# A hybrid encoder layer: first loads in smaller pieces, shorter routing, and eleven lower weight parts on GpSimd

## Chip, cores and metric

The kernel runs on one core of one Trainium2 chip. The metric is the device time of one execution in microseconds (us). Engines are named TensorE (PE; PEld is its weight load), VectorE (DVE), ScalarE (ACT), GpSimd (POOL) and SyncE (SP), which issues nearly all the DMA transfers here.

## The reference, cut to what matters

One layer over 256 tokens of 2048 float32 values. A projection of the normed input feeds a gated causal convolution (31 taps, 1024 channels) and a differential attention (8 heads); both go through an output projection and are added to the input. Then each token is routed to one of 4 groups and there to 2 of 8 experts.

```python
u = rms_norm(h, norm1_g) @ w_in                     # 2048 x 5120
y_conv = conformer_conv(u[..., :2048], ...)         # a * sigmoid(b), 31 taps, layer norm, silu
y_attn = diff_attention(u[..., 2048:], ...)         # chunk mask, softmax(0) - lam * softmax(1)
h = h + concat([y_conv, y_attn]) @ w_out            # 2048 x 2048
t = rms_norm(h, norm2_g)
g_idx = argmax(t @ w_group + b_group)
top_v, top_i = top_k((t @ w_router + b_router)[g_idx], 2)
for e in range(32):
    out += combine[:, e:e + 1] * ((silu(t @ w_gate[e]) * (t @ w_up[e])) @ w_down[e])
return h + out
```

## The kernel before

**Front part.** The input projection has 80 steps and the output projection 32, numbered 0 to 111. A step has 256 rows of the contraction and 512 output columns for both token tiles (128 tokens each). Both operands are split into an upper part, rounded to fp32r, and a lower part, the rest; a step is twelve products of 128x512, three for each block of 128 rows and each token tile: upper by upper (L721), upper by lower weight (L722), lower by upper weight (L723). `split` makes a step's weight parts: ScalarE copies the upper part (L672), VectorE subtracts for the lower (L673). There are three buffers for them (`SP`, pairs 18 to 20), and `split` runs two steps ahead of the products. For the first eight steps it also splits two blocks of x (`split_x`, L263).

The work that depends on a finished projection stands in small generators ("units": gated products and conv taps, keys, queries, values, attention, its norm, conv norm and output). The program's order on TensorE, ScalarE, VectorE and GpSimd is the order in which the code is written: ahead of each step `vector_phase` lets units run on ScalarE and VectorE, as far as a room in microseconds for each engine lasts (`PACE_A`, `PACE_V`), and fills VectorE's room with conv taps, `TAP` = 0.40 each; behind each step `tensor_phase` lets units put products on TensorE. Where a step needs a unit that is not done, `idle_until` (L248) runs phases with room `IDLE` and two filler products each. Two such places matter: step 88, the second half of attention in the output projection, and step 96, where the conv output enters it.

```python
room["D"] = min(room["D"], SAVE) + d + room["P"]
fill(room["D"] - sum(u["n"][1] for u in units if may(u, "D")))
```

**Routing.** `finish` adds the last output parts, transposes the result and multiplies it by the router. Then VectorE picks group and experts (L764 to L789), TensorE counts positions, and `dispatch` (L847) builds one-hot matrices that gather tokens into 64 slots an expert.

**Expert stage.** 16 pairs of experts; each pair's gate, up and down weights come in 12 transfers of 2 MB through a ring of nine buffers (`E_RING`), which are those of the front part, and a transfer is issued when its buffer has been read.

Of the kernel before, what the change touches and what calls it, by code (L numbers as in the profile page):

```python
# [9 lines left out]
F32 = mybir.dt.float32  # L10
# [3 lines left out]
U32 = mybir.dt.uint32  # L14
# [22 lines left out]
IDLE = 2.5  # L37
# [5 lines left out]
WARM, WARM2 = 12, 3  # L43
SAVE, NTMP, NORM1_AT = 0.0, 6, 5
# [13 lines left out]
def block_kernel(ctx, tc, x, xT, par, w_in, w_out, w_gu, w_dn, out):  # L58
# [22 lines left out]
    nc.scalar.dma_start(pr[:, p1:], par[:, p1:])  # L81
# [22 lines left out]
    xs = cst.tile([128, NT, D], F32, name="xs")  # L104
    for t in range(NT):
        nc.sync.dma_start(xs[:, t], x[t * 128:(t + 1) * 128])
    win += [stream(IN_PAIRS[2], w_in[2])]
# [18 lines left out]
    place = cst.tile([128, NT, EPG], U32, name="place")  # L126
    nc.gpsimd.iota(place, pattern=[[0, NT], [1, EPG]], base=0, channel_multiplier=0)
# [3 lines left out]
    nc.vector.memset(eps_c, EPS)  # L131

# [107 lines left out]
    def keep_warm(n):  # L240

        if n and free_banks:
            i, ps = bank()
            for _ in range(n):
                nc.tensor.matmul(ps[:, :128], ident, ident, start=True, stop=True)
            free_banks.append(i)

    def idle_until(done):  # L248
# [3 lines left out]
        while not done():  # L252
            vector_phase(IDLE, IDLE)
            keep_warm(IDLE_MM)
# [178 lines left out]
    def queries(half, ps):  # L433
# [4 lines left out]
        for t in range(NT):  # L438
            yield "A", 1.3, 2
# [53 lines left out]
    def attend(t, g, s, st):  # L493
# [15 lines left out]
        for r in range(2):  # L509
            yield "D", 1.0, 0  # L510
            b0, v = pv[r]
            nc.vector.memset(v[0:64, :, K - 64:K], NEG)
# [706 lines left out]
```

## Time and profile before

| what | value |
|---|---|
| time, median of 3 runs (lowest to highest) | 1305.32 us (1304.71 to 1306.32) |
| the profiled execution's own time | 1305.24 us |
| its span | 1303.3 us |
| TensorE busy | 1231.6 us, 94% |
| VectorE, ScalarE, GpSimd busy | 515.6, 291.7, 46.8 us |
| first expert product | 385.59 us |
| DMA rate, mean over the span | 360 GB/s |

Times inside the profile count from the span's start. A busy time is the union of an engine's instructions; products overlap in the pipeline, so TensorE's pace is read from the distance of their starts. Lines (L672) are those of the kernel before; the changed kernel's numbers differ.

### The profile page before, as it was taken

To read this page: it belongs to the slowest core of one execution; us is meant where nothing else is said; L and a number is where in the kernel's file an instruction comes from. 1 tells how busy PE (TensorE), PEld (TensorE's weight loads), DVE (VectorE), ACT (ScalarE), POOL (GpSimd) and SP (SyncE) were. 2 spreads that over 40 slices of the span, in tenths; PEclk is the share of its full clock that TensorE was granted. 3 is DMA by queue.
4 is the path that set the end of the run, shared out by engine and by line. 5 is a ranking of instruction groups with operands and counts; after the bars stand their busy time and mean duration, and the time that the engine had idled before them with its cause. 6 is when DMAs were issued, how large, how long until landed. Compare 5 with 4: busy or idle time off the path is not lost.

```text
span 1303.3 us, 15071 instructions
## 1 busy us (share of the span) xinstructions
PE 1231.6 (94%) x6291; PEld 700.8 (54%) x6291; DVE 515.6 (40%) x996; ACT 291.7 (22%) x516; POOL 46.8 (4%) x116
## 2 busy tenths in 40 slices
PE   7999999989999999999999898999989898998997
PEld 5888888878884353553535435252525344352533
DVE  6899989897541030330303213030303123030313
ACT  6446565645421010110101101010101001010101
POOL 1001211120000000000000000000000000000000
PEclk9999999989999999999999999999999999999999
DMA  9454534665749999999999999999999999999996
GB/s 385 173 184 180 194 137 187 256 260 212 273 183 420 426 426 429 427 427 426 429 427 428 427 427 428 427 428 427 427 426 430 426 428 425 429 428 427 427 426 246
DMA packets 37032, 469.29 MB, mean 360 GB/s; under 512 B 4192, under 2 KB 4960, under 8 KB 8160
## 3 DMA queue, kind: packets, MB, share of 16 engines
q1 hardware_dynamic: 35808, 466.63, 86.1%
q10 hardware_dynamic: 1152, 1.65, 0.4%
q8 instruction: 51, 0.84, 0.3%
q14 instruction: 21, 0.17, 0.0%
HBM read 466.17 MB, written 2.10 MB: 359 GB/s over the span
## 4 chain that ended last, share of the span: by engine, by line
PE 65%; DMA 31%; DVE 2%; ACT 1%; POOL 1%; issue 0%; SPq 0%
DMA v<-in_w_gu_dram 28%; PE b L891 13%; PE b L929 13%; PE b L872 8%; PE b L722 7%; PE b L723 7%; PE b L721 7%; PE b L956 4%; DMA v<-in_w_dn_dram 3%; PE b L505 1%; PE b L633 1%; PE b L907 0%; ACT t L430 0%; DMA v<-in_w_in_dram 0%; PE b L561 0%; DVE u L673 0%
## 5 line engine op out<-in xcount | busy, mean ns | idle before, releaser
L891 PE MATMUL b<-v,u 128*64 128x512 f32 x2048 | 452.5, 594 | 45.4 <-DMA v<-in_w_gu_dram 45.3
L891 PEld LDWEIGHTS b<-v,u 128*64 128x64 f32 x2048 | 142.8, 137 | 349.7 <-issue 264.4
L900 DVE TENSOR_TENSOR hid<-sil,b 64x512 f32<-64x512 f32 x32 | 21.9, 685 | 517.5 <-ACT sil L899 517.4
L929 PE MATMUL b<-v,hT 128*64 128x512 f32 x992 | 217.2, 594 | 1.3 <-DMA v<-in_w_dn_dram 0.8
L721 PE MATMUL b<-u,v 128*128 128x512 f32 x448 | 179.0, 400 | 8.4 <-ACT u L672 8.4
L722 PE MATMUL b<-u,v 128*128 128x512 f32 x448 | 175.6, 392 | 1.1 <-DVE u L673 1.1
L723 PE MATMUL b<-u,v 128*128 128x512 f32 x448 | 175.7, 392 | 0.0
L673 DVE TENSOR_TENSOR u<-v,u 128x1024 fp32r<-128x1024 f32 x112 | 137.4, 1228 | 47.1 <-ACT u L672 46.7
L672 ACT ACTIVATE u<-v 128x1024 fp32r<-128x1024 f32 x112 | 119.0, 1063 | 140.3 <-PE b L723 108.9
L929 PEld LDWEIGHTS b<-v,hT 128*64 128x64 f32 x992 | 69.7, 137 | 134.2 <-issue 131.6
L899 ACT ACTIVATE sil<-b,sv 64x512 f32<-64x512 f32 x32 | 21.8, 682 | 527.7 <-PE b L891 503.1
L872 PEld LDWEIGHTS b<-dg,xs 128*128 128x128 f32 x1024 | 121.1, 192 | 14.7 <-issue 11.7
L872 PE MATMUL b<-dg,xs 128*128 128x128 f32 x1024 | 125.5, 276 | 0.5 <-ACT hT L909 0.2
L937 ACT ACTIVATE u<-b,sv 128x512 fp32r<-128x512 f32 (+1 forms) x66 | 44.4, 674 | 244.5 <-PE b L929 193.3
L721 PEld LDWEIGHTS b<-u,v 128*128 128x128 f32 x448 | 84.9, 189 | 25.2 <-ACT u L672 8.4
L325 DVE SCALAR_TENSOR_TENSOR v<-v,pr 128x255 f32<-128x255 f32 (+14 forms) x240 | 97.1, 464 | 0.0
L722 PEld LDWEIGHTS b<-u,v 128*128 128x128 f32 x448 | 84.8, 189 | 18.9 <-DVE u L673 2.2
L723 PEld LDWEIGHTS b<-u,v 128*128 128x128 f32 x448 | 84.6, 189 | 17.9
L938 DVE SCALAR_TENSOR_TENSOR u<-b,sv,u 128x512 fp32r<-128x512 f32 (+1 forms) x66 | 48.2, 732 | 109.4 <-ACT u L937 109.4
L956 PE MATMUL b<-u,dwT 128*128 128x512 f32 (+2 forms) x264 | 76.7, 412 | 0.3 <-DVE u L957 0.3
L874 DVE TENSOR_TENSOR u<-b,g2v 128x512 f32<-128x512 f32 x64 | 44.3, 692 | 29.7 <-PE b L872 29.2
L957 DVE TENSOR_TENSOR u<-u,b 128x512 f32<-128x512 f32 (+2 forms) x62 | 41.2, 664 | 29.6 <-PE b L956 29.6
(202 smaller groups left out, 553.7 us busy)
## 6 DMA issues: line engine op xcount, KB each, us to landing
v<-in_w_gu_dram SPq DMA_DIRECT2D x125, 2048.0 KB, 32.5
v<-in_w_dn_dram SPq DMA_DIRECT2D x60, 2048.0 KB, 34.7
v<-in_w_in_dram SPq DMA_DIRECT2D x18, 2048.0 KB, 8.0
v<-in_w_out_dram SPq DMA_DIRECT2D x8, 2048.0 KB, 8.6
v<-in_w_gu_dram SPq DMA_DIRECT2D x6, 1024.0 KB, 12.3
v<-in_w_dn_dram SPq DMA_DIRECT2D x5, 1024.0 KB, 8.0
v<-in_w_in_dram SPq DMA_DIRECT2D x8, 512.0 KB, 8.9
v<-in_xT_dram SPq DMA_DIRECT2D x4, 512.0 KB, 8.5
```

What stands on the lines that cost most here:

```text
L325: nc.vector.scalar_tensor_tensor(cacc[:, b, d:], hb[:, b, :S - d], ck[:, b, j:j + 1], cacc[:, b, d:], op0=ALU.mult, op1=ALU.add)
L672: nc.scalar.activation(sp[:, 0], w, AF.Copy)
L673: nc.vector.tensor_tensor(sp[:, 1], w, sp[:, 0].bitcast(F32), op=ALU.subtract)
L721: nc.tensor.matmul(o, lh, sp[:, 0, k2], start=first and k2 == 0, stop=False)
L722: nc.tensor.matmul(o, lh, sp[:, 1, k2], start=False, stop=False)
L723: nc.tensor.matmul(o, ll, sp[:, 0, k2], start=False, stop=last and k2 == 1)
L872: nc.tensor.matmul(tv[:, k], xs[:, t, (k0 + k) * 128:(k0 + k + 1) * 128], dg[:, t].rearrange("p i c -> p (i c)"), start=t == 0, stop=t == 1)
L891: nc.tensor.matmul(gu[i][h:h + 64], tT[:, kb, i * C:(i + 1) * C], w[:, k2, g], start=kb == 0, stop=kb == KB - 1, skip_group_check=True)
L929: nc.tensor.matmul(ps[64 * i:64 * i + 64], hT[:, f, i], columns(wd[i], f), start=f == 0, stop=f == 3, skip_group_check=True)
L937: nc.scalar.activation(y[:, 0, a:b], ps[:, :b - a], AF.Copy, scale=sv[:, 0:1])
L938: nc.vector.scalar_tensor_tensor(y[:, 1, a:b], ps[:, :b - a], sv[:, 0:1], y[:, 0, a:b].bitcast(F32), op0=ALU.mult, op1=ALU.subtract)
L956: nc.tensor.matmul(ps[:, :b - a], dwT[:, t], y[:, k, a:b], start=k == 0, stop=k == 1)
```

## The change

1. First loads: x comes in two pieces of 0.26 MB for the first four blocks; the second part of the parameters moves from ScalarE's queue to SyncE's, behind the weights of step 3; the third weight pair comes in halves around x itself. ScalarE's table load is put ahead of the data by a dummy instruction. Eleven filler products stand ahead of the first step. Step 0's weight parts are made in two halves.
2. Eleven lower parts (steps 14, 16, ..., 34) are made by GpSimd. From step 12 to 69 `split` runs three steps ahead, and from step 11 to 73 the buffer of the conv output (`CY`) gives two more buffers for weight parts.
3. The first norm starts at step 9 instead of 5. Idle turns give VectorE 1.3 instead of 2.5. The mask is filled by ScalarE; the squares of the first half of the queries are summed by ScalarE.
4. The last two steps run by token tile, so that tile 0 is transposed earlier.
5. Routing works on all 32 experts' logits with a penalty for the groups not chosen, instead of first picking 8; `dispatch` builds its four one-hot blocks by one instruction.

The core of the diff:

```diff
+WARM0, WARM, WARM2 = 11, 12, 3
+POOL_STEPS, MORE_AT = range(14, 36, 2), 11
+SAVE, NTMP, NORM1_AT = 0.0, 6, 9
...
-    nc.scalar.dma_start(pr[:, p1:], par[:, p1:])
...
     for q in range(4):
-        nc.sync.dma_start(xT_s[:, 4 * q:4 * q + 4], xTv[:, 4 * q:4 * q + 4])
         for p in range(2):
             cs = slice(p * 1024, (p + 1) * 1024)
+            if q == 0:
+                nc.sync.dma_start(xT_s[:, 2 * p:2 * p + 2], xTv[:, 2 * p:2 * p + 2])
+            elif p == 0:
+                nc.sync.dma_start(xT_s[:, 4 * q:4 * q + 4], xTv[:, 4 * q:4 * q + 4])
             nc.sync.dma_start(win[q // 2][:, q % 2, cs], w_in[q // 2][:, q % 2, cs])
+        if q == 1:
+            nc.sync.dma_start(pr[:, p1:], par[:, p1:])
...
+    nc.scalar.activation(dummy, eps_c, AF.Copy)
...
+            vector_phase(IDLE, IDLE_V)
+            keep_warm(warm)
...
-            nc.vector.memset(v[0:64, :, K - 64:K], NEG)
+            nc.scalar.activation(v[0:64, :, K - 64:K], mean_w[0:64, None, :64].to_broadcast([64, nh, 64]), AF.Copy,
+                                 scale=NEG * DC)
...
+        if j == MORE_AT:
+            cs = pair(CY, [128, 2, 2, 2, 512], F32R)
+            for i in range(2):
+                more_sp.append(cs[:, i])
+                last_user["c", i] = -9
+        i = min([i for i in last_user if (i != SP[0] or j < 96) and (i in SP or j < 74)], key=lambda x: last_user[x])
...
+        if j == 0:
+            for k2, kb in enumerate(kx):
+                split_x(kb)
+                nc.scalar.activation(sp[:, 0, k2], w[:, k2], AF.Copy)
+                nc.vector.tensor_tensor(sp[:, 1, k2], w[:, k2], sp[:, 0, k2].bitcast(F32), op=ALU.subtract)
+        else:
+            nc.scalar.activation(sp[:, 0], w, AF.Copy)
+            eng = nc.gpsimd if j in POOL_STEPS else nc.vector
+            if eng is nc.gpsimd:
+                room["D"] += 1.22
+            eng.tensor_tensor(sp[:, 1], w, sp[:, 0].bitcast(F32), op=ALU.subtract)
...
+    keep_warm(WARM0, mean_w)
...
+            if MORE_AT < j < 70:
+                ahead = 3
...
+            if j >= len(steps) - 2:
+                if j == len(steps) - 2:
+                    products(j, [0])
+                    products(j + 1, [0])
...
-    nc.vector.tensor_tensor(pick, lg[:, :, NG:].rearrange("p t (g e) -> p t g e", g=NG), goh4, op=ALU.mult)
-    nc.vector.tensor_reduce(el, pick.rearrange("p t g e -> p t e g"), axis=AX.X, op=ALU.add)
+    nc.vector.tensor_scalar(goh, goh, -1.0, -NEG, op0=ALU.add, op1=ALU.mult)
+    nc.vector.tensor_tensor(el.rearrange("p t (g e) -> p t g e", g=NG), lg[:, :, NG:].rearrange("p t (g e) -> p t g e", g=NG),
+                            goh[:, :, :, None].to_broadcast([128, NT, NG, EPG]), op=ALU.add)
...
-        for t in range(NT):
-            for i in range(2):
-                nc.vector.tensor_scalar(dg[:, t, i], slots, pc(t, i), None, op0=ALU.is_equal)
+        nc.vector.tensor_tensor(dg, slots[:, None, None, :].to_broadcast([128, NT, 2, C]),
+                                pc[:, :, :, None].to_broadcast([128, NT, 2, C]), op=ALU.is_equal)
```

How it moves instructions, at three places. On VectorE, around the gated products of the third half of the gate (steps 24 to 26). Before: L673 is a step's lower part, L325 a conv tap, L338 a gated product.

```order
L673 TENSOR_TENSOR u_648<-v_429,u_648 128x1024
L325 SCALAR_TENSOR_TENSOR v_121<-v_121,pr 128x233 x2
L325 SCALAR_TENSOR_TENSOR v_121<-v_121,pr 128x232 x2
L673 TENSOR_TENSOR u_673<-v_429,u_673 128x1024
L325 SCALAR_TENSOR_TENSOR v_121<-v_121,pr 128x231 x2
L338 SCALAR_TENSOR_TENSOR t_655<-b_494,rstd_118,t_655 128x256
L338 SCALAR_TENSOR_TENSOR t_657<-b_495,rstd_118,t_657 128x256
L673 TENSOR_TENSOR u_694<-v_511,u_694 128x1024
```

And now, where these are L706, L334 and L347, up to the lower part of step 29:

```order
L706 TENSOR_TENSOR v_341<-v_416,v_341 128x1024
L334 SCALAR_TENSOR_TENSOR v_124<-v_124,pr 128x238
L334 SCALAR_TENSOR_TENSOR v_124<-v_124,pr 128x237 x2
L334 SCALAR_TENSOR_TENSOR v_124<-v_124,pr 128x236 x2
L334 SCALAR_TENSOR_TENSOR v_124<-v_124,pr 128x235
L347 SCALAR_TENSOR_TENSOR t_660<-b_502,rstd_121,t_660 128x256
L347 SCALAR_TENSOR_TENSOR t_662<-b_503,rstd_121,t_662 128x256
L706 TENSOR_TENSOR u_698<-v_493,u_698 128x1024
```

Every second lower part is gone from VectorE, and six to eight taps stand between two of those that are left.

On VectorE, in the wait ahead of step 88, behind the rsqrt of the last attention norm; L591 and L593 scale the attention output (L577 and L579 before), L602 makes its lower part (L588), L615 adds an output part (L601), L379 subtracts the conv mean (L370). Now:

```order
L615 TENSOR_TENSOR xs<-xs,b_2395 128x512
L591 TENSOR_TENSOR oy<-oy,rs_2254 128x4
L593 TENSOR_TENSOR t_2460<-b_2270,oy 128x512
L591 TENSOR_TENSOR oy<-oy,rs_2286 128x4
L593 TENSOR_TENSOR t_2466<-b_2408,oy 128x512
L334 SCALAR_TENSOR_TENSOR v_124<-v_124,pr 128x230
L334 SCALAR_TENSOR_TENSOR v_124<-v_124,pr 128x229 x2
L334 SCALAR_TENSOR_TENSOR v_124<-v_124,pr 128x228 x2
L334 SCALAR_TENSOR_TENSOR v_124<-v_124,pr 128x227 x2
L602 SCALAR_TENSOR_TENSOR v_1663<-b_2471,qg,v_1663 128x4x128
L334 SCALAR_TENSOR_TENSOR v_124<-v_124,pr 128x226
L602 SCALAR_TENSOR_TENSOR v_1663<-b_2484,qg,v_1663 128x4x128
```

Before, all taps stood ahead of the second tile's scaling, and the conv mean was subtracted ahead of its lower part; now the last tap and the subtraction stand behind it.

On ScalarE, the conv output ahead of step 96. Before: L387 loads a table behind the root of the conv variance, L672 is a step's upper part (here of steps 91 to 93), L407 and L408 make the output of the first of four channel groups.

```order
L387 ACT_TABLE_LOAD
L387 ACTIVATE dummy<-eps_c 128x1
L672 ACTIVATE u_2548<-v_2077 128x1024
L672 ACTIVATE u_2571<-v_2201 128x1024
L672 ACTIVATE u_2590<-v_2201 128x1024
L407 ACTIVATE v_121<-v_121,pr 128x256 x2
L408 ACTIVATE v_2558<-v_121 128x512
```

And now (L396, L701, L416, L417; L395 is the root), with the upper parts of steps 95 and 96:

```order
L395 ACTIVATE t_2600<-b_2586,eps_c 128x256
L396 ACT_TABLE_LOAD
L396 ACTIVATE dummy<-eps_c 128x1
L701 ACTIVATE u_2619<-v_2199 128x1024
L701 ACTIVATE u_2658<-v_2337 128x1024
L416 ACTIVATE v_124<-v_124,pr 128x256 x2
L417 ACTIVATE v_2629<-v_124 128x512
```

Before, the other groups followed with the upper parts of steps 94 and 95 between them; now the three others follow at once, and behind them stands the upper part of step 97.

## Rows read from the trace of the kernel before

**Rows 1.** Busy time by stretch: columns PE, PEld, DVE, ACT, POOL, clock, DMA, GB/s

```profile
17.88:279.60 261.72, 261.29 (x1230) 218.07 (x1229) 235.29 (x460) 152.68 (x295) 36.54 (x91) 1.00 0.55 209
281.00:295.68 14.68, 9.18 (x50) 8.23 (x48) 12.15 (x27) 7.15 (x17) 4.62 (x13) 0.77 0.41 150
295.68:370.14 74.46, 74.43 (x365) 62.05 (x364) 44.63 (x57) 36.81 (x50) 0.00 (x0) 1.00 0.61 230
390.00:1280.00 890.00, 841.07 (x4368) 380.40 (x4366) 191.98 (x361) 78.86 (x126) 0.00 (x0) 1.00 1.01 427
```

**Rows 2.** Time line of SyncE's queue, DMA issues (start, us, what)

```profile
370.48 0.43 SPq L991 DMA_DIRECT2D v<-in_w_gu_dram  x1
...
387.59 5.46 SPq L989 DMA_DIRECT2D v<-in_w_dn_dram  x4
```

**Rows 3.** Time line of the start (start, us, engine, line, what, count, idle before)

```profile
4.80 1.28 ACT L265 ACT_TABLE_LOAD   x1 [4.80 <-DMA v<-in_xT_dram]
...
6.10 0.91 ACT L265 ACTIVATE v<-v,pr 128x256 fp32r<-128x256 f32 x2
...
7.29 1.06 ACT L672 ACTIVATE u<-v 128x1024 fp32r<-128x1024 f32 x1 [0.29 <-DMA v<-in_w_in_dram]
...
8.40 0.80 PE L721 MATMUL b<-u,v 128*128 128x512 f32 x1 [8.40 <-ACT u L672]
...
10.28 0.80 PE L722 MATMUL b<-u,v 128*128 128x512 f32 x1 [1.08 <-DVE u L673]
...
15.11 0.39 PE L721 MATMUL b<-u,v 128*128 128x512 f32 x1
...
17.88 0.39 PE L721 MATMUL b<-u,v 128*128 128x512 f32 x1
```

**Rows 4.** Time line, GpSimd and VectorE at once

```profile
7.99 1.15 POOL L301 TENSOR_TENSOR pr<-pr 128x576 f32<-128x576 f32 x1 [2.70 <-DMA pr<-in_par_dram]
...
8.38 1.84 DVE L673 TENSOR_TENSOR u<-v,u 128x1024 fp32r<-128x1024 f32 x1 [0.86 <-ACT u L672]
...
108.79 1.23 DVE L673 TENSOR_TENSOR u<-v,u 128x1024 fp32r<-128x1024 f32 x1 [0.27 <-ACT u L672]
108.90 1.20 POOL L148 TENSOR_TENSOR kh<-kh,kv 128x16 f32<-128x16 f32 x1
...
113.92 0.22 POOL L148 TENSOR_TENSOR kh<-kh,kv 128x16 f32<-128x16 f32 x1
```

**Rows 5.** Time line, VectorE's taps, a gated product and TensorE's transposes

```profile
53.42 1.64 DVE L325 SCALAR_TENSOR_TENSOR v<-v,pr 128x250 f32<-128x250 f32 x4
...
84.55 0.87 DVE L338 SCALAR_TENSOR_TENSOR t<-b,rstd,t 128x256 f32<-128x256 f32 x2
...
86.82 0.60 PE L346 MATMUL b<-ident,t 128*128 128x128 f32 x4
```

**Rows 6.** Time line ahead of step 88 (L721 from 295.68 is its first product)

```profile
279.57 1.05 PE L561 MATMUL b<-v,t 128*128 128x128 f32 x8
...
287.90 2.07 PE L366 MATMUL b<-v,mean_w 128*128 128x256 f32 x4 [5.50 <-DVE v L325]
...
292.41 3.62 PE L381 MATMUL b<-t,mean_w 128*128 128x256 f32 x16
...
293.76 0.75 DVE L588 SCALAR_TENSOR_TENSOR v<-b,qg,v 128x512 fp32r<-128x512 f32 x1 [1.27 <-ACT v L586]
...
295.68 0.58 PE L721 MATMUL b<-u,v 128*128 128x512 f32 x1
```

**Rows 7.** Time line, conv output on VectorE and ScalarE

```profile
301.39 1.74 DVE L390 RECIPROCAL t<-t 128x256 f32<-128x256 f32 x1
...
306.29 1.09 ACT L407 ACTIVATE v<-v,pr 128x256 f32<-128x256 f32 x2 [0.95 <-DVE v L403]
...
307.41 0.63 ACT L408 ACTIVATE v<-v 128x512 fp32r<-128x512 f32 x1
```

**Rows 8.** Time line, one-hot builds ahead of the first gather

```profile
377.60 1.39 DVE L852 TENSOR_SCALAR dg<-slots,pos 128x64 f32<-128x64 f32 x8
```

More of the change, by code (lines that the diff above doesn't have):

```diff
@@ L125, in block_kernel @@
                    allow_small_or_imprecise_dtypes=True)
-    place = cst.tile([128, NT, EPG], U32, name="place")
-    nc.gpsimd.iota(place, pattern=[[0, NT], [1, EPG]], base=0, channel_multiplier=0)
+    place = cst.tile([128, NT, NE], U32, name="place")
+    nc.gpsimd.iota(place, pattern=[[0, NT], [1, NE]], base=0, channel_multiplier=0)
     dummy = cst.tile([128, 1], F32, name="dummy")
@@ L244, in keep_warm, with idle_until @@
             for _ in range(n):
-                nc.tensor.matmul(ps[:, :128], ident, ident, start=True, stop=True)
+                w = ident if w is None else w
+                nc.tensor.matmul(ps[:, :128], w, w, start=True, stop=True)
             free_banks.append(i)
-    def idle_until(done):
+    def idle_until(done, warm=IDLE_MM):
         nonlocal now
@@ L715, in block_kernel, with products @@
                 ps[pk] = [bank() for _ in range(NT)]
-            for k2 in range(2):
-                for t in range(NT):
-                    ts = slice(t * 128, (t + 1) * 128)
-                    o, sp = ps[pk][t][1], halves[j]
-                    lh, ll = lhs[0][:, kb0 + k2, ts], lhs[1][:, kb0 + k2, ts]
-                    nc.tensor.matmul(o, lh, sp[:, 0, k2], start=first and k2 == 0, stop=False)
-                    nc.tensor.matmul(o, lh, sp[:, 1, k2], start=False, stop=False)
-                    nc.tensor.matmul(o, ll, sp[:, 0, k2], start=False, stop=last and k2 == 1)
+            def products(j, tiles):
+                _, _, kb0, _, pk, first, last = steps[j]
+                for k2 in range(2):
+                    for t in tiles:
+                        ts = slice(t * 128, (t + 1) * 128)
+                        o, sp = ps[pk][t][1], halves[j]
+                        lh, ll = lhs[0][:, kb0 + k2, ts], lhs[1][:, kb0 + k2, ts]
+                        nc.tensor.matmul(o, lh, sp[:, 0, k2], start=first and k2 == 0, stop=False)
+                        nc.tensor.matmul(o, lh, sp[:, 1, k2], start=False, stop=False)
+                        nc.tensor.matmul(o, ll, sp[:, 0, k2], start=False, stop=last and k2 == 1)
+            if j >= len(steps) - 2:
+                if j == len(steps) - 2:
+                    products(j, [0])
+                    products(j + 1, [0])
+                    tensor_phase(2)
+                    now += 1
+                    start(finish(pk[2], 0, ps[pk][0]), 1, quick=True)
+                else:
+                    products(j - 1, [1])
+                    tensor_phase(0)
+                    now += 1
+                    vector_phase(PACE_A, PACE_V)
+                    products(j, [1])
+                    tensor_phase(0)
+                    now += 1
+                    start(finish(pk[2], 1, ps[pk][1]), 1, quick=True)
+                continue
+            products(j, range(NT))
             tensor_phase(2)
@@ L747, in block_kernel @@
         nc.scalar.activation(dummy, eps_c, AF.Sqrt)
-        idle_until(lambda: not units)
+        idle_until(lambda: not units, 0)
     keep_warm(WARM)
```

75 lines of the change are left out of this document (33 added, 42 removed).

## The prediction

> **What bounds the kernel now.** I read the busy times by stretch first, then SyncE's queue, then the time line of three places: the start, the wait ahead of the output projection's second part, and the routing. From 390 us to 1280 us the DMA engines are busy all the time (share 1.01, 427 GB/s), and TensorE has pauses (841 of 890 us) [rows 1]. So the expert stage runs at the pace of its weights, whatever an engine does in it. What starts that stream? SyncE issues the last transfer for which there is a free buffer at 370.48, and the next at 387.59 [rows 2], when the first expert products have read their first buffer. From there the stream never stops. So every microsecond by which the front part ends earlier comes off the end, one for one, and nothing in the expert stage itself can add to it.
>
> In the front part TensorE is the bound. From 17.88, where the third step of the input projection (step 2) begins, to 279.6 it is busy 261.29 of 261.72 us, and from 295.68 to 370.14 for 74.43 of 74.46; VectorE has 235.29 us in the first of these stretches [rows 1], which is nearly full, but it is in time. In between lies the one hole: 281.0 to 295.68, where TensorE is busy 9.18 us at a granted clock of 0.77, and much of that is filler. So the change can win time at the start (17.9 us for two steps), in the hole, and in the routing. Between 17.88 and 279.6 it can only lose.
>
> **The start.** Before, ScalarE waits until 4.80 for the first 0.52 MB of x and then loads its table for 1.28; the first weights let it go at 7.29, the first product stands at 8.40, the second waits for VectorE until 10.28, then the products start 0.44 apart (11 intervals to 15.11), and step 2 begins at 17.88, the products now 0.23 apart (12 from 15.11 to 17.88) [rows 3]. [...]
>
> Changed: the table load stands ahead of the data, the second parameter load (0.59 MB) behind the weights of step 3, and x comes in 0.26 MB pieces. Ahead of the first weights' last byte there are now 0.80 MB instead of 1.65; at 427 GB/s [rows 1] this is 2.0 us, so they land at 7.29 - 2.0 = 5.3. The small parameter load on ScalarE's queue is as before, so I leave ScalarE's first product at 4.80. Then: scaling of one x block 0.46 (half of 0.91 [rows 3]), copy of half a weight tile 0.6 (half of 1.06 and a little), the same again, and step 1 with 0.91 + 1.06: its copy ends at 8.9. VectorE's lower part, 1.23 [rows 5], ends at 10.15. There step 1's second product starts, 11 more at 0.23 follow, and step 2 begins at 12.8 instead of 17.88: **-5.1**. This takes TensorE at the high level from step 0 on: eleven filler products run from 1.3 to 6.0 (each is recorded as two of 128 columns, together one of 256, and four of those took 2.07 with the last one's tail at the low level [rows 6], 0.43 each); before, TensorE ran from 10.28 to 15.11 until its level rose. Bounds: -6.0 if the parameters land sooner, -3.5 if the level rises only in step 1 (some 8 products at 0.2 more).
>
> **Eleven lower parts on GpSimd.** TensorE did not wait for lower parts, so nothing is won directly; the question is what GpSimd costs VectorE. No row shows a 1024-wide subtraction on GpSimd. The nearest: 128x576 took 1.15, and a 128x16 one 0.22 [rows 4], so 1.65 ns an element and 1.9 us for 1024. [...]
>
> Next, both engines at once. VectorE's lower part that started at 8.38 while GpSimd's 128x576 ran until 9.14 took 1.84 instead of 1.23; and a GpSimd instruction of 0.22 took 1.20, because VectorE's lower part from 108.79 ended at 110.02 [rows 4]. So one stands still while the other reads two inputs. [...]
>
> With that, the move takes 1.23 off VectorE and puts 1.9 of standing still on it, eleven times in 22 steps. Does TensorE see it? The first place is the transposes of the third gated half ahead of step 27, which need two VectorE results; before, these were ready 1.4 us early (84.55 + 0.87 against 86.82) [rows 5]. By the new order VectorE has, from its first conv tap (behind the transposes ahead of step 14) to there, 43 taps of 0.39, five lower parts of 1.2, four gated products of 0.44 and 6 or 7 stops of 1.9: 16.8 + 6.0 + 1.8 + 12.4 = 37.0. TensorE needs 13 steps of 2.72 and four transposes, 35.8, less 1.7 until the first tap: 34.1. VectorE is 2.9 late; some of the stops fall into its gated products, which read one input from PSUM and need not stop, so I take **+2.0**. Three steps of lead and five buffers keep the products themselves supplied (TensorE is three steps, 8.2 us, behind). Bounds: 0 (no stop) and +6 (2.5 us each, and again at the keys ahead of step 37).
>
> Nor do more taps get done for it: the credit that each moved part gives is cut to zero ahead of the next step's taps, as room is limited to SAVE = 0. By the order 68 taps stand ahead of the lower part of step 36 where 80 stood before, partly as the first norm starts at step 9 instead of 5.
>
> **The hole and the conv output.** Before, the last attention product group starts at 279.57 and step 88 at 295.68. Useful work in the hole: L366 0.9 (2.07 at the low level), L381 3.5, four transposes 0.4 [rows 6], so 14.7 - 4.8 = 9.9 are lost. In the new order the last group stands one step earlier, and VectorE has behind its squares: four taps, two adds, the rsqrt (on GpSimd, 12 instructions of 0.22 [rows 4] and the step to the next, 3.4), two 512-wide products, seven taps, the low part of the first tile, a tap, the low part of the second. With 0.39 a tap and 0.7 for 512 wide [rows 5, 6] the low parts stand 12.9 and 14.1 after the group's start, step 88, whose third and sixth products need them, ends at 15.7, and without waiting it would end at 7.2: 8.5 lost. Now the variance products (L390, L381 before) stand ahead of step 92 and no longer ahead of step 88, so the conv output has four steps (10.9) to step 96 where it had eight. VectorE's reciprocal stands behind the lower part of step 95, whose upper part waits for the buffer of step 92: it starts 5.6 after the variance. Reciprocal and Newton take 3.1, the first scaling 0.65 [rows 7], so ScalarE begins at 9.3; then all four groups, 1.7 each, stand on ScalarE ahead of the upper part of step 97. Low part of group 0: 13.6, step 96 waits 2.4. Upper part of 97: 9.3 + 6.8 + 1.1 = 17.2, lower 18.4, where it was wanted at 16.3: 2.1 more. Sum 8.5 + 4.5 - 9.9 = **+3.1**. Bounds: -4 (the conv output hidden, a shorter rsqrt) and +5.
>
> **End of the front part.** The four one-hot builds ahead of the first gather, half of 1.39 [rows 8], become one of 128x256, 0.44 as the gated product of that size [rows 5]: -0.26. Of the routing two 64-wide instructions of some 0.25 go, one comes, and four read 64 or 32 elements instead of 16 or 8: -0.1. The last two steps by token tile: tile 0 is transposed 0.44 earlier and delays the last product by as much; VectorE's chain behind it is the same: 0. Together **-0.4** (0 to -1).
>
> **At nothing:** the squares of half the queries (1.6 more on ScalarE each, 0.7 less on VectorE) and the mask's fill on ScalarE, which has 153 of 262 us [rows 1]; were ScalarE late, TensorE would wait up to 2 us at step 50. Fewer taps in idle turns is in the walk above. The 15 later one-hot builds lie beside the stream.
>
> **Sum:** -5.1 + 2.0 + 3.1 - 0.4 = -0.4. The profiled execution took 1305.24, the median is 1305.32: forecast **1304.8**, no change that a measurement can tell (0.2% is 2.6 us).
>
> **Rivals.** *GpSimd does not stop VectorE, and the conv output fits (faster).* Its reads fall into VectorE's pauses (10% of that stretch [rows 1]), and the upper part of step 97 finds ScalarE free. Then 2.0 and 4.5 go: 1298.3. For it: GpSimd's short instructions cost VectorE's taps nothing visible. Against it: the 1.84.
>
> *The stop is longer (slower).* Writing fp32r and reading two full inputs, a part takes 3.0 us on GpSimd; VectorE is then 6.5 x 1.1 = 7.2 later at step 27, and TensorE waits there for the gated products: 1312.0. It decides from 2.4 us a part on, where 6.5 x 0.5 = 3.3 more give 1308.1; at 2.6 it is 1309.4. [...]
>
> *The start gives less.* If the level stays low through step 1 and the weights land late, the start brings -2.5: 1307.4, still within 0.2%.
>
> *The change does what it says:* freed time on VectorE closes the conv early and the hole shrinks to the rsqrt, 5 us: 1305.2 - 5.1 + 2.0 - 5 - 0.4 = 1296.7. The order speaks against it: 225 taps stand ahead of the lower part of step 86, 228 before.
>
> **Chances.** Forecast 0.36, faster rival 0.32, slower 0.18, weak start 0.08, early conv 0.06. So faster 0.38, same 0.44, slower 0.18. The range takes in the early conv, and the slower rival to 2.6 us a part: 1296.5 to 1309.5.
>
> **What would show it.** Step 2 beginning at 12 to 14 us; GpSimd's parts near 1.9 us and VectorE's instructions beside them longer by about that; a wait of TensorE ahead of step 27 for a gated product; waits at steps 88, 96 and 97 of 8, 2 and 2 us; the first expert product less than 1 us earlier. It is wrong if the hole is under 5 us, if GpSimd's parts take over 2.6, or if the expert stage's stream is interrupted.

## The result and the profile after

The changed kernel takes **1311.95 us** (median of 4 runs, 1311.29 to 1313.16) against 1305.01 of the kernel before in the same measurement: ratio 1.0054, 95% interval 1.0042 to 1.0067. It is slower by 7 us. The forecast was 1304.8 with a range up to 1309.5, so it was wrong in sign and outside its range. The profiled execution took 1311.9, its span is 1310.1 (1303.3 before).

First the busy times by stretch, for the same four stretches as [rows 1] (step 2 to the hole, the hole, step 88 to the end of the output projection, the expert stage). Columns as there: length, then PE, PEld, DVE, ACT, POOL busy, clock, DMA share, GB/s.

```profile
13.47:283.57 270.10, 265.70 (x1243) 220.38 (x1242) 242.14 (x443) 160.91 (x348) 70.78 (x100) 0.99 0.56 215
283.57:292.18 8.61, 4.83 (x24) 4.35 (x23) 5.82 (x17) 2.00 (x3) 3.36 (x17) 0.69 0.42 170
292.18:374.99 82.81, 78.93 (x374) 65.09 (x374) 49.46 (x64) 38.98 (x55) 0.00 (x0) 0.97 0.53 194
398.00:1290.00 892.00, 842.81 (x4375) 381.29 (x4372) 188.11 (x319) 78.87 (x126) 0.00 (x0) 1.00 1.01 427
```

The last line is as before: the stream of expert weights runs without a break, and what the front part loses is lost at the end. The other three differ. TensorE, which had 0.43 us of idle time in the first stretch before (261.29 of 261.72 busy), now has 4.4 us. VectorE, from which eleven instructions were taken, is busy 242 us instead of 235 (in a stretch 8 us longer). And behind the hole TensorE is idle for 3.9 of 82.8 us, where it was idle for 0.03 of 74.5.

**The start** (time line, rows of ScalarE and TensorE), to be held against [rows 3]:

```profile
1.19 1.28 ACT L139 ACT_TABLE_LOAD   x1 [1.19 <-PEq L1259]
...
5.91 0.63 ACT L698 ACTIVATE u<-v 128x512 fp32r<-128x512 f32 x1 [0.92 <-DMA v<-in_w_in_dram]
...
6.60 0.68 PE L761 MATMUL b<-u,v 128*128 128x512 f32 x1 [0.32 <-ACT u L698]
...
10.80 0.50 PE L762 MATMUL b<-u,v 128*128 128x512 f32 x1 [0.42 <-DVE u L706]
...
13.47 0.39 PE L761 MATMUL b<-u,v 128*128 128x512 f32 x1
```

Step 2 begins at 13.47 instead of 17.88, with products 0.23 apart from step 0 on. That is 4.4 us sooner (forecast 5.1). The weights let ScalarE go at 5.91, where the prediction had 5.3.

**GpSimd's parts** (time line of GpSimd, VectorE and TensorE; L706 is the lower part, L347 the gated product, L334 a tap, L355 the transposes of a gated half):

```profile
43.25 2.42 POOL L706 TENSOR_TENSOR u<-v,u 128x1024 fp32r<-128x1024 f32 x1 [28.19 <-ACT u L701]
45.62 3.36 POOL L706 TENSOR_TENSOR v<-v,v 128x1024 fp32r<-128x1024 f32 x1
...
56.51 2.45 POOL L706 TENSOR_TENSOR u<-v,u 128x1024 fp32r<-128x1024 f32 x1 [4.18 <-ACT u L701]
60.14 2.50 POOL L706 TENSOR_TENSOR v<-v,v 128x1024 fp32r<-128x1024 f32 x1 [1.18 <-ACT v L701]
70.10 4.28 POOL L706 TENSOR_TENSOR u<-v,u 128x1024 fp32r<-128x1024 f32 x1 [7.47 <-ACT u L701]
...
44.15 2.60 DVE L706 TENSOR_TENSOR u<-v,u 128x1024 fp32r<-128x1024 f32 x1 [1.67 <-ACT u L701]
46.67 0.86 DVE L347 SCALAR_TENSOR_TENSOR t<-b,rstd,t 128x256 f32<-128x256 f32 x2
...
56.62 6.68 DVE L334 SCALAR_TENSOR_TENSOR v<-v,pr 128x252 f32<-128x252 f32 x6
63.22 0.86 DVE L347 SCALAR_TENSOR_TENSOR t<-b,rstd,t 128x256 f32<-128x256 f32 x2
...
47.20 0.83 PE L355 MATMUL b<-ident,t 128*128 128x128 f32 x4 [0.93 <-DVE t L347]
...
63.75 0.83 PE L355 MATMUL b<-ident,t 128*128 128x128 f32 x4 [2.07 <-DVE t L347]
...
65.17 0.63 PE L761 MATMUL b<-u,v 128*128 128x512 f32 x1
...
68.53 0.39 PE L763 MATMUL b<-u,v 128*128 128x512 f32 x1
```

Read the sixth row with the first: VectorE's lower part starts at 44.15, while GpSimd's first part runs, and takes 2.60 instead of 1.23 [rows 4]. Behind it on VectorE stand the two gated products, and TensorE waits 0.93 for them ahead of step 14. The six taps from 56.62 take 6.68 instead of some 2.5 (four took 1.64 in [rows 5]), because two parts of GpSimd (56.51 and 60.14) fall into them; the next gated products start at 63.22, and TensorE waits 2.07 ahead of step 19. After that wait its products start 0.43 apart from 65.17 to 68.53 (granted clock 0.64 from 63.7 to 68.5): eight intervals take 3.36 where they take 1.82 at 0.227, another 1.5 us. The part at 70.10 shows the other side: five taps of VectorE run end to end, and GpSimd's part takes 4.28.

Before the change, VectorE's results for the transposes ahead of step 19 were ready at 63.22, 1.4 us before TensorE came to them (L338 is the gated product, L346 the transposes):

```profile
62.35 0.87 DVE L338 SCALAR_TENSOR_TENSOR t<-b,rstd,t 128x256 f32<-128x256 f32 x2
...
64.59 0.60 PE L346 MATMUL b<-ident,t 128*128 128x128 f32 x4
```

**The hole and the conv output** (time line, TensorE and VectorE; L575 the last product group of attention, L429 the transposes of its normalised output, L375 the second part of the conv's mean, L390 its variance, L399 the reciprocal, L419 a low part of the conv's output):

```profile
279.27 1.05 PE L575 MATMUL b<-v,t 128*128 128x128 f32 x8
...
287.34 1.11 PE L429 MATMUL b<-ident,t 128*128 128x128 f32 x4 [3.38 <-DVE t L593]
...
296.38 1.02 PE L375 MATMUL b<-v,mean_w 128*128 128x256 f32 x4
...
305.46 3.62 PE L390 MATMUL b<-t,mean_w 128*128 128x256 f32 x16
...
312.94 1.23 DVE L706 TENSOR_TENSOR u<-v,u 128x1024 fp32r<-128x1024 f32 x1 [3.53 <-ACT u L701]
...
314.42 1.75 DVE L399 RECIPROCAL t<-t 128x256 f32<-128x256 f32 x1
...
322.47 0.50 PE L763 MATMUL b<-u,v 128*128 128x512 f32 x1 [1.58 <-DVE v L419]
...
326.00 0.50 PE L761 MATMUL b<-u,v 128*128 128x512 f32 x1 [0.97 <-ACT u L701]
...
327.26 0.50 PE L762 MATMUL b<-u,v 128*128 128x512 f32 x1 [0.76 <-DVE u L706]
```

In [rows 6] the mean and the variance stood inside the hole. Now the mean stands behind step 88, the variance ahead of step 92, the reciprocal behind VectorE's lower part at 312.94. TensorE waits for the conv's low part in step 96 (1.58) and for both parts of step 97's weights (0.97 and 0.76).

**The tail**: the first gather's two one-hot builds, and the issue that starts the stream.

```profile
385.40 0.76 DVE L902 TENSOR_TENSOR dg<-slots,pos 128x256 f32<-128x256 f32 x2
```

```profile
395.29 3.74 SPq L1040 DMA_DIRECT2D v<-in_w_dn_dram  x3
```

The two builds take 0.76 where eight took 1.39 [rows 8]. The issue that waits for the first expert products starts at 395.29 instead of 387.59 [rows 2]: 7.7 us later, and the stream follows.

### The profile page after: what moved, and what is told of

Its sections match the earlier page's. It is cut to its first block, busy times and chain, and to the rows that moved or that the text cites. A ratio compares the mean times of both kernels' runs of the same rounds, so it can differ in the third digit from the quotient of the medians.

```text
span 1310.1 us, 15097 instructions
## 1 busy us (share of the span) xinstructions
PE 1239.9 (95%) x6305; PEld 705.5 (54%) x6305; DVE 512.5 (39%) x922; ACT 297.5 (23%) x560; POOL 79.0 (6%) x127
## 4 chain that ended last, share of the span: by engine, by line
PE 58%; DMA 32%; DVE 6%; ACT 1%; issue 1%; POOL 1%; SPq 0%; ACTq 0%; DVEq 0%
DMA v<-in_w_gu_dram 28%; PE b L942 13%; PE b L980 13%; PE b L923 8%; PE b L763 5%; PE b L762 5%; PE b L761 5%; PE b L1007 4%; DMA v<-in_w_dn_dram 3%; DVE v L334 2%; DMA v<-in_w_in_dram 2%; DVE u L706 1%; PE b L517 1%; ACT u L701 1%; PE b L958 0%
## 5 line engine op out<-in xcount | busy, mean ns | idle before, releaser
L761 PE MATMUL b<-u,v 128*128 128x512 f32 x344 | 139.5, 406 | 1.3 <-ACT u L701 1.0
L763 PE MATMUL b<-u,v 128*128 128x512 f32 x344 | 135.6, 394 | 2.1 <-DVE v L419 1.6
L762 PE MATMUL b<-u,v 128*128 128x512 f32 x344 | 135.9, 395 | 1.2 <-DVE u L706 1.2
L706 DVE TENSOR_TENSOR u<-v,u 128x1024 fp32r<-128x1024 f32 x78 | 100.9, 1296 | 45.6 <-ACT u L701 45.6
L701 ACT ACTIVATE u<-v 128x1024 fp32r<-128x1024 f32 x85 | 89.8, 1062 | 87.7 <-PE b L763 78.3
L334 DVE SCALAR_TENSOR_TENSOR v<-v,pr 128x255 f32<-128x255 f32 (+14 forms) x240 | 109.3, 515 | 0.0
L763 PEld LDWEIGHTS b<-u,v 128*128 128x128 f32 x344 | 65.4, 190 | 17.3 <-DVE v L419 2.0
L762 PEld LDWEIGHTS b<-u,v 128*128 128x128 f32 x344 | 65.7, 191 | 15.2 <-DVE u L706 1.9
L761 PEld LDWEIGHTS b<-u,v 128*128 128x128 f32 x344 | 65.5, 190 | 14.6 <-ACT u L701 1.4
## 6 DMA issues: line engine op xcount, KB each, us to landing
v<-in_w_in_dram SPq DMA_DIRECT2D x2, 1024.0 KB, 13.6
```

The source lines that it names most:

```text
L334: nc.vector.scalar_tensor_tensor(cacc[:, b, d:], hb[:, b, :S - d], ck[:, b, j:j + 1], cacc[:, b, d:], op0=ALU.mult, op1=ALU.add)
L701: nc.scalar.activation(sp[:, 0], w, AF.Copy)
L706: eng.tensor_tensor(sp[:, 1], w, sp[:, 0].bitcast(F32), op=ALU.subtract)
L761: nc.tensor.matmul(o, lh, sp[:, 0, k2], start=first and k2 == 0, stop=False)
L762: nc.tensor.matmul(o, lh, sp[:, 1, k2], start=False, stop=False)
L763: nc.tensor.matmul(o, ll, sp[:, 0, k2], start=False, stop=last and k2 == 1)
```

## The experiments

Each kernel was run with the kernel before on the same chip. The tables give its median, and by how much the first product of a step of the projections starts later (+) or sooner (-) on TensorE than before the change, one trace against one trace.

| kernel | median us | ratio, 95% | step 12 | 20 | 80 | 88 | 92 | 100 |
|---|---|---|---|---|---|---|---|---|
| the change | 1311.95 | 1.0042 to 1.0067 | -4.88 | +0.99 | +2.38 | -3.49 | +1.94 | +7.86 |
| e1 no part on GpSimd | 1306.49 | 1.0005 to 1.0023 | -5.36 | -4.19 | -4.26 | -8.67 | -5.19 | +2.42 |
| e2 old norm and room | 1315.96 | 1.0070 to 1.0097 | +0.54 | +5.72 | +7.78 | +6.42 | +12.07 | +11.55 |
| e3 start alone | 1305.16 | 0.9993 to 1.0011 | -0.30 | -0.30 | -0.31 | -0.02 | -0.02 | 0.00 |
| e4 GpSimd alone | 1310.50 | 1.0026 to 1.0054 | -0.71 | +4.80 | +6.01 | +4.71 | +4.68 | +4.71 |

Theory A was what the trace of the change suggested: GpSimd's parts cost 6 to 7 us, the rest of the loss is the conv output. Theory B: the parts cost nothing, the later first norm, the shorter idle turns and the squares on ScalarE do.

**e1, the change without parts on GpSimd**

```diff
-POOL_STEPS, MORE_AT = range(14, 36, 2), 11
+POOL_STEPS, MORE_AT = (), 11
```

> The changed kernel with all lower parts on VectorE again; everything else stays, the two extra buffers and the three steps of lead too. Theory A (GpSimd's parts cost some 6 to 7 us: the waits ahead of steps 14 and 19, the low level after them and the keys; the rest of the loss is the conv output): 1305 to 1307 us, step 20 within 0.7 us of -4.9 against the kernel before, no wait over 0.5 us ahead of steps 14 and 19. Theory B (the parts on GpSimd cost nothing; the loss comes with the later first norm, the shorter idle turns and the squares on ScalarE): 1311 to 1313 us, with the waits ahead of 14 and 19 still there.

1306.49 us: 5.5 us of the 7 went, and theory B fell. Step 20 stands at -4.19. From step 12 to 14 it loses 1.16 us, of which 0.44 are no delay: the transposes of the first gated half stood ahead of step 12 before and stand ahead of step 14 now. The wait there is 0.42. But the table shows something that the whole change had hidden: from step 88 on this kernel gives back 11.1 us (-8.67 to +2.42). The hole is 4.4 us shorter than before the change, mostly because the variance's 3.6 us of products have left it, and behind it they and what waits for them cost 11.1: a net loss of 6.7 between steps 80 and 100. The longest waits of TensorE from 270 to 340 us (engine, its line, what it waited for: us, times, longest; L593 scales the attention output, L615 adds an output part from the bank that the next step needs):

```profile
PE b L429 <- DVE t L593: 3.1, 1, 3.1
PE b L761 <- DVE xs L615: 2.5, 1, 2.5
```

**e2, the change with the old first norm and the old room**

```diff
-IDLE, IDLE_V = 2.5, 1.3
+IDLE, IDLE_V = 2.5, 2.5
-SAVE, NTMP, NORM1_AT = 0.0, 6, 9
+SAVE, NTMP, NORM1_AT = 0.0, 6, 5
```

> The changed kernel with the first norm at step 5 and 2.5 us of room for VectorE in an idle turn, as before. By the order 240 taps then stand ahead of the lower part of step 86 (225 in the change) and the variance products ahead of step 88 again (92 in the change). Theory A: the conv output's loss of 5.5 us goes for the most part, the waits that GpSimd's parts make stay: 1306 to 1308.5 us, step 20 still at about +1 us against the kernel before. Theory B, if the first norm and the idle turns are the cause: 1300 to 1302 us. If GpSimd alone is the cause of all: 1311 to 1313 us.

1315.96, slower than every theory had it. The table says where: the start's gain is gone by step 12. Two numbers changed at once here; e3, e5 and e6 take them apart.

**e3, the start alone in the kernel before** (the loads in smaller pieces, the early table load, the eleven fillers, step 0 in halves; NORM1_AT stays 5)

> The kernel before with the changed start alone: the smaller first loads, the early table load, the eleven first filler products, step 0 in halves. Theory A: the 4.4 us at step 2 reach the end, 1300 to 1301.5 us. Rival (VectorE sets the pace behind the start, and the norm's data land too late for step 5): the gain is gone by step 20, 1304 to 1306 us.

1305.16, no change: the gain is gone by step 12 (-0.30), as the rival had it. VectorE's time line in this kernel, and TensorE's next wait (L287 squares x for the first norm, L701 is the lower part):

```profile
29.83 2.29 DVE L287 SCALAR_TENSOR_TENSOR v<-xs 128x2048 f32<-128x2048 f32 x1 [3.23 <-DMA xs<-in_x_dram]
...
32.05 1.22 DVE L701 TENSOR_TENSOR u<-v,u 128x1024 fp32r<-128x1024 f32 x1
```

```profile
33.32 0.50 PE L757 MATMUL b<-u,v 128*128 128x512 f32 x1 [2.46 <-DVE u L701]
```

VectorE stands still for 3.23 us until the second half of x has landed, and the lower part that TensorE needs is queued behind it; with a second wait of 0.37 this makes 2.8 of the 3.7 us that are lost from step 2 to step 12. So the steps come sooner, but the norm's data do not: the later first norm is no side edit, it is what lets the start's gain through.

**e4, GpSimd's parts alone in the kernel before** (with the lead of three steps and the two buffers)

> The kernel before with the eleven lower parts on GpSimd, the three steps of lead and the two extra buffers, and nothing else of the change. Theory A: waits ahead of steps 14 to 20 as in the changed kernel and a lower level after them, GpSimd's parts at 2.4 us and more: 1309.5 to 1312.5 us. Theory B: 1304 to 1306 us.

1310.50, as theory A had it. From step 12 to 80 the parts, with their credit, cost 6.7 us (-0.71 to +6.01), 5.5 of it by step 20; behind step 88 nothing is lost here.

| kernel | median us | ratio, 95% | step 12 | 20 | 80 | 88 | 92 | 100 |
|---|---|---|---|---|---|---|---|---|
| e5 no GpSimd, old room | 1299.74 | 0.9952 to 0.9979 | -5.13 | -4.36 | -4.60 | -4.69 | -4.71 | -4.66 |
| e6 GpSimd, old room | 1312.18 | 1.0041 to 1.0068 | -5.04 | -0.77 | +3.04 | +0.59 | +5.20 | +7.92 |
| e7 no taps | 1303.56 (one run) | | -5.19 | -3.16 | -3.91 | -11.17 | -6.64 | -0.73 |
| e8 a best version | 1299.95 | 0.9955 to 0.9979 | -4.63 | -4.03 | -3.89 | -4.35 | -4.35 | -4.33 |
| e9 e5, parts on GpSimd | 1306.21 | 1.0000 to 1.0018 | -5.40 | -1.36 | +1.52 | +2.37 | +2.38 | +2.41 |
| e10 e5, last six parts | 1301.54 | 0.9967 to 0.9985 | -5.15 | -4.38 | -3.08 | -3.30 | -3.29 | -3.28 |
| e11 e8, rsqrt on VectorE | 1308.40 | 1.0016 to 1.0039 | -4.56 | -4.01 | -3.95 | +2.01 | +2.24 | +3.70 |
| e12 e8, one such rsqrt | 1306.40 | 0.9999 to 1.0017 | -3.68 | -3.21 | -3.13 | -5.09 | -1.09 | +1.69 |

**e5, e1 with the old room in idle turns**

```diff
-IDLE, IDLE_V = 2.5, 1.3
+IDLE, IDLE_V = 2.5, 2.5
-POOL_STEPS, MORE_AT = range(14, 36, 2), 11
+POOL_STEPS, MORE_AT = (), 11
```

> The run without GpSimd's parts again, and VectorE's room in an idle turn at 2.5 us as before; the first norm stays at step 9. By the order both parts of the conv norm then stand ahead of step 88, as before the change. Theory C (without GpSimd the change gains 4.3 us until step 84, and the 1.3 us of room in idle turns gives 6.7 of it away behind the hole, because the conv norm is not through when the hole ends): 1300 to 1302 us, step 100 at -4 to -5 against the kernel before. Rival D (the conv's loss comes from the taps that the later first norm pushes back, 219 against 228 ahead of step 86): 1304 to 1307 us.

1299.74: theory C. It is faster than both kernels, and the start's gain goes to the end undiminished (-4.36 at step 20, -4.66 at step 100). Ahead of step 86 it has as few taps as e1 (219), so rival D is out: one number, how many taps VectorE may issue in an idle turn, decides by 6.7 us whether the conv's norm gets through inside the hole.

**e6, the change with the old room**

```diff
-IDLE, IDLE_V = 2.5, 1.3
+IDLE, IDLE_V = 2.5, 2.5
```

> The changed kernel with only VectorE's room in an idle turn at 2.5 us again, GpSimd's parts in place. By the order the second part of the mean then stands ahead of step 88 (89 in the change) and the variance ahead of 89 (92). Theory C: GpSimd's share (+2.4 against the kernel before at step 84) stays, the conv's 5.5 go down to 1 or 2: 1307 to 1309 us. Rival D: 1310.5 to 1312.5 us.

1312.18, the number of rival D, whose reason e5 had just refuted; theory C missed by 3 us. With GpSimd's parts in place the old room brings nothing. So the two edits don't add: the parts cost 5.5 us with 1.3 us of room (the change against e1) and 12.4 with 2.5 (e6 against e5). This led to theory E, tried in e9.

**e7, the change without the taps** (only the last tap of each conv block is left, so the conv is not computed)

> The changed kernel without the conv's taps but the last one of each block, so that VectorE has much idle time: what does a part on GpSimd take, and does TensorE still wait ahead of steps 14 and 19? Theory A (VectorE and GpSimd hold each other up; a GpSimd part alone is 2.0 to 2.4 us): the shortest parts as before at 2.39, most of them under 2.6 us, and no wait over 0.5 us ahead of steps 14 and 19. Rival (a part is long by itself, 2.9 us and more): most of them over 2.8 us.

GpSimd's groups by shape from 30 to 110 us (busy, mean ns, idle time before):

```profile
L703 POOL TENSOR_TENSOR u<-v,u 128x1024 fp32r<-128x1024 f32 x7 | 17.0, 2432 | 45.9 <-ACT u L698 45.9
L703 POOL TENSOR_TENSOR v<-v,v 128x1024 fp32r<-128x1024 f32 x4 | 10.5, 2634 | 7.8 <-ACT v L698 7.8
```

Beside the taps these groups have means of 2767 and 2995 ns in the change. Nine of the eleven parts now take 2.39 to 2.41: that is a part by itself, and theory A was right. The wait ahead of step 19 is gone, the one ahead of step 14 is not (1.2 us, expected under 0.5): there no taps are left to be stopped, and in the change it is VectorE's lower part that takes 2.60 (44.15). And though VectorE has far less to do, the steps from 80 to 100 still lose 3.2 us (-3.91 to -0.73) of the 5.5 in the change, and the variance stands ahead of step 92 as there. That points to the norm's place in the order for more than half of the conv's loss, and not to a full VectorE.

**e8, a version meant to beat both** (no part on GpSimd, no third step of lead, old room, NORM1_AT = 8)

> A version meant to be under both kernels: the changed start, routing, squares and mask, the first norm at step 8, all lower parts on VectorE two steps ahead, no extra buffers, 2.5 us of room for VectorE in idle turns. By the order 231 taps stand ahead of the lower part of step 86 (228 before). Theory C: 1300 to 1301.5 us. Rival (at step 8 VectorE waits for the norm's data as it did at step 5): 1303 to 1305 us.

1299.95, as expected, and level with e5: the extra buffers, the lead and one step in the first norm's place make no difference that shows.

**e9, e5 with the parts on GpSimd and no credit**

```diff
-            if eng is nc.gpsimd:
-                room["D"] += 1.22
```

> The run without GpSimd's parts and with 2.5 us of room (1299.74 us), with the eleven parts put on GpSimd again but without the 1.22 us of credit, so that no tap, no product and no idle turn changes its place: only the engine of the parts differs. Theory E (two engines in each other's way at steps 14 to 20 and at the keys, some 7 us; the conv's loss comes from the plan that the credit makes): 1305.5 to 1308 us, step 20 at +0 to +1.5 against the kernel before, no loss between steps 88 and 100. Rival F (the credit's plan is the whole loss): 1299.5 to 1302 us. Rival G (the engine alone costs all the 12.4 us between this run's model and the one with GpSimd and 2.5 us of room): 1310.5 to 1313 us.

1306.21: theory E by the time; step 20, expected at +0 to +1.5, stands at -1.36. Against e5 only the engine of eleven instructions differs, and that costs 6.5 us, nearly all of it ahead of step 88 (6.1 at step 80) and none behind it (+2.37 to +2.41). The busy times of e5 from 13 to 279 us, and of e9 from 13 to 285.1, since e9 is late by 6.1 us at the end of the stretch; so the same instructions are counted on VectorE, 458 and, without the eleven, 447:

```profile
13.00:279.00 266.00, 264.71 (x1254) 220.78 (x1252) 235.82 (x458) 162.82 (x350) 41.79 (x93) 1.00 0.57 218
```

```profile
13.00:285.10 272.10, 265.20 (x1253) 220.35 (x1251) 244.55 (x447) 162.90 (x350) 70.44 (x104) 1.00 0.56 214
```

VectorE lost eleven parts of 1.22, 13.4 us, and is busy 8.7 us more: the eleven parts stretched its other work by some 22 us, 2.0 each. So it falls behind from part to part. Its last result for the second gated half comes 5.7 us later than in e5, that for the third 9.3. Here is the third half, the gated product and the transposes that need it, first in e5, then in e9:

```profile
80.61 0.48 DVE L347 SCALAR_TENSOR_TENSOR t<-b,rstd,t 128x256 f32<-128x256 f32 x1
...
85.29 0.60 PE L355 MATMUL b<-ident,t 128*128 128x128 f32 x4
```

```profile
89.89 0.47 DVE L347 SCALAR_TENSOR_TENSOR t<-b,rstd,t 128x256 f32<-128x256 f32 x1
...
90.42 0.44 PE L355 MATMUL b<-ident,t 128*128 128x128 f32 x2 [1.74 <-DVE t L347]
```

In e5 the result is ready at 81.09 and the last two of the four transposes, which need it, start at 85.5: TensorE has 4.4 us to spare. At the second half it has 2.8, at the first none. In e9 VectorE is 9.3 us late at the third half and TensorE itself 3.0, so some 1.9 are left over, and TensorE waits 1.74. Its waits in e9 from 40 to 125 us:

```profile
PE b L355 <- DVE t L347: 4.8, 3, 1.7
PE b L429 <- DVE t L483: 0.8, 1, 0.8
```

Three gated halves (ahead of steps 14, 20 and 28) and one of the keys' results, 5.6 of the 6.1 us. The other 6 us, between e9 and e6, are the credit alone: 1.5 of them stand at step 80 already (+3.04 against +1.52), 4.0 come between steps 80 and 100. Here is TensorE around the hole, first in e6, then in e9 (L254 is filler, L390 the variance):

```profile
279.93 1.05 PE L575 MATMUL b<-v,t 128*128 128x128 f32 x8
280.73 0.47 PE L761 MATMUL b<-u,v 128*128 128x512 f32 x1
...
289.11 1.11 PE L429 MATMUL b<-ident,t 128*128 128x128 f32 x4 [4.49 <-DVE t L593]
...
300.36 3.62 PE L390 MATMUL b<-t,mean_w 128*128 128x256 f32 x16
```

```profile
281.05 1.05 PE L575 MATMUL b<-v,t 128*128 128x128 f32 x8
281.94 0.60 PE L429 MATMUL b<-ident,t 128*128 128x128 f32 x4
...
289.58 2.08 PE L375 MATMUL b<-v,mean_w 128*128 128x256 f32 x4 [5.71 <-DVE v L334]
...
294.78 3.62 PE L390 MATMUL b<-t,mean_w 128*128 128x256 f32 x16
```

With the credit the last product group of attention stands a step sooner (ahead of step 87), its norm ends in fewer idle turns (10 filler products instead of 12 in the order), and the variance falls behind step 88. Without it, it stands inside the hole, as before the change.

**e10, e9 with the last six parts only**

```diff
-POOL_STEPS, MORE_AT = range(14, 36, 2), 11
+POOL_STEPS, MORE_AT = range(24, 36, 2), 11
```

> As the run without credit, with only the last six parts on GpSimd (steps 24 to 34); the five of steps 14 to 22 are VectorE's. Theory E (the cost lies where a gated product waits behind a part, at steps 14 and 19): those waits go, step 27 or the keys keep 1 to 2.5 us: 1300.5 to 1302.5 us. Rival (each part costs the same wherever it stands): six elevenths of the loss of the run with eleven.

1301.54, 1.8 us over e5, where six elevenths of 6.5 would be 3.5. The step table has 1.5 us at step 80. TensorE's waits from 40 to 125 us are at the keys and ahead of step 28:

```profile
PE b L429 <- DVE t L483: 0.8, 1, 0.8
PE b L355 <- DVE t L347: 0.2, 1, 0.2
```

The third gated half's last result is 4.7 us later than in e5 (9.3 in e9), hardly more than the 4.4 that TensorE has to spare there. From step 20 to 80 e9 loses 2.9 us and e10 1.3, with the same six parts in that stretch. So a part has no fixed price: it is paid when the delay that the parts have added up on VectorE is more than TensorE has to spare at the next result that it needs, and in e9 the first five parts had used that up.

**e11 and e12, shortening the hole by the rsqrt on VectorE** (in e8, for both tiles of the last attention group, and for the first alone)

```diff
+        last = g == 1 and t in LAST
-        ro = rstd_bits(..., "o", nc.gpsimd)
-        yield "W", 2
+        ro = rstd_bits(..., "o", nc.vector if last else nc.gpsimd)
+        if last:
+            room["D"] -= 2.4
+        yield "W", 0 if last else 2
```

> The best version (first norm at step 8, no part on GpSimd, 2.5 us of room) with the reciprocal roots of the last two attention norms on VectorE instead of GpSimd, to shorten the hole ahead of step 88: 9 Newton instructions of 0.2 us without a step between engines instead of 12 of 0.28 and three steps. If that chain sets the hole's end: 1296.5 to 1298.5 us. If the taps that VectorE puts back for it set the end: 1299 to 1301.5 us.

> The same with only the first tile's norm of that group on VectorE. By the order the variance products then stand ahead of step 89 and no longer of 88. If the chain sets the hole's end: 1297.5 to 1299.5 us; if the conv's norm behind step 88 costs as it did with 1.3 us of room: 1301 to 1305 us.

1308.40 and 1306.40: both lost, and both are slower than their expectations had it. In e11 the rsqrt stands ahead of the taps, and the hole is 6 us longer (-3.95 to +2.01); which of the moved instructions makes the 6 us was not tried. In e12 the hole is 2 us shorter, the variance falls behind step 88, and 6.8 us are paid back by step 100: e1 and e6 again, by a third edit.

## Why the prediction was wrong, point by point

- **The bound and the one-for-one rule**: right. The first expert product comes 7.7 us later (385.59 to 393.29), the span is 6.8 longer, the stream has no pause. In every run the end moves as step 100 does, to within 1.2 us; from the first expert product to the end the traces take 916.7 to 918.5.
- **The start, -5.1**: -4.4 at step 2, in its bounds, the high level (products 0.23 apart) from step 0 on included (the -4.9 at step 12 holds the 0.44 of transposes that moved behind it). But the sum took this term as independent, and e3 shows that it isn't: with the old first norm it is worth nothing. And the late first norm itself holds up the first gated half: 0.5 to 1.1 us between steps 12 and 80 in e1, e5 and e8, less the same 0.44, which the prediction had at nothing.
- **GpSimd's parts, +2.0**: this is the step that failed. It is 6.2 us in the change (the change gains 7.26 of delay from step 12 to 80, e1 1.10), 6.7 in e4, 6.4 in e9 against e5. The backlog that the prediction reckoned with is there, and near its size: VectorE's net load grew by 8.7 us in e9, where the prediction's figures give 7.4, and a stop costs 2.0 where it had 1.9. What failed is where TensorE meets the backlog. The prediction called the transposes ahead of step 27 the first place and took VectorE as in time up to its first tap, behind the transposes ahead of step 14. But the lower part ahead of the first gated products is stopped already (2.60 instead of 1.23), and TensorE waits 0.93 ahead of step 14 and 2.07 ahead of step 19; after the second wait its products start 0.43 apart for 3.36 us, which costs 1.5 us more, and the keys take another 1.2. Ahead of step 27, the one place that went into the sum, the change has no wait. The prediction's own figures have the wait at step 19: 15 taps, a lower part, two gated products and three stops, 13.6 us, against five steps less 1.7, 11.9. The size was the smaller fault: a part takes 2.40 alone (e7), not the 1.9 scaled from GpSimd's 128x576. The upper bound, +6, held "2.5 us each, and again at the keys"; it is about what came.
- **That one engine stands still while the other reads**: right for the lower parts and the taps, and longer than the rows before could show. [rows 4] had 1.84 instead of 1.23; now a tap of 0.46 beside a part takes up to 2.6 and a lower part up to 3.37 (86.53, beside the part from 86.42 to 88.81), and GpSimd's part takes up to 4.28 while taps follow end to end. That the gated products, one of whose inputs lies in PSUM, need not stop was shown by no row before; in the change two of them take 0.86 from 46.67 on, beside the part from 45.62 to 48.98, as without one (0.87 in [rows 5]). Which property of an instruction decides whether it stops was not tried.
- **"The credit is cut to zero"**: wrong. It can cancel debts of the room, and e9 against e6 gives it a price of 6 us. The prediction had seen by the order that the last attention group moved up a step, and not that the credit moved it.
- **The hole and the conv output, +3.1**: +5.5 from step 80 to 100. The mechanism was right (the variance ahead of step 92, the conv's output four steps later, waits in 96 and at 97's weights); the hole's share was -1.4 and is -0.2 at step 93 (+2.38 to +2.14), the conv's share was 4.5 and is 5.7. The prediction left the smaller idle room out as "in the walk above". It is one of two edits each of which is enough to drop the norm out of the hole: e5 and e1 have 1299.74 and 1306.49, e9 and e6 have 1306.21 and 1312.18.
- **The tail, -0.4**: the eleven kernels with the new routing all take 21.1 us from step 110 to the first expert product, where the kernel before takes 21.2: 0.15 sooner, less than half of the forecast. To the end of the span they gain 0.5 us on average, with single traces from +0.66 to -1.15, which can't be told from nothing.
- **At nothing**: the squares and the mask on ScalarE did no harm that shows, since e5 keeps them and its steps stand still from 20 to 100. They weren't tried apart.
- **The rivals**: the slower one had the time (1312.0) and its condition (from 2.4 us a part on), but not the place: no wait ahead of step 27 in the change. That the time fits is luck: GpSimd gave 4.2 us more than the sum had, the conv norm 2.4, and the start fell short. The faster one's time, 1298.3, is near e5, and not by its mechanism: the parts have to go, not to be harmless.

So the 7 us are, by steps: -4.4 at the start, +0.7 around the late first norm, +6.2 from the parts on GpSimd with their credit (only e9 has the engine without it, 6.4), +5.5 from the conv norm behind the hole, and 1.0 back at the end. What the change is worth without the parts on GpSimd and with the old room is e5's or e8's 5 us, nearly all of it the start with the norm moved (-4.66 and -4.33 at step 100).

## What to carry to other kernels

The work moved from VectorE to GpSimd freed no VectorE time here: it took 13.4 us off and put some 22 on. Follow the delay from part to part, and hold it against what TensorE has to spare at each result that it needs, from the first one on; one place in the middle is not enough, and neither is the sum of busy times. When busy times of two runs are compared, shift the stretch by the delay between them: the same stretch of 13 to 279 us would have shown e9's VectorE only 2.7 us busier instead of 8.7. An edit that makes steps come sooner needs its data to come sooner too; look at the first wait for a DMA on any engine in that stretch. And where a planner's credits set the order, a small number can move a chain across a boundary: read where the chain stands in the order, then price both places, in e1 and e12 the hole became 4.4 and 2.0 us shorter, and the steps behind it 11.1 and 6.8 longer.

## What the runs showed of the hardware

The stop is nearly complete in both directions: one VectorE tap of 0.46 us takes 2.6 beside a GpSimd part of 2.4, also the tap with a single tensor input (L331, two of them in 2.81 where they take 0.73 in e3), and a series of VectorE taps makes the same part 4.28. Short GpSimd instructions suffer too: the first instruction of the last rsqrt in e5, 0.20 us alone at 265.32, took 1.36 beside taps at 277.61.
